# Second block's mixer: two gate products of the convolution ahead of the projections, and an accumulator of its own

## The chip, the cores and the metric

One core of a Trainium2 chip runs the whole program. The metric is device time in microseconds (us) of one execution. TensorE (PE) multiplies matrices and writes to PSUM, VectorE (DVE) and ScalarE (ACT) work on elements, SyncE (SP) issues the transfers. Each engine runs its own queue of instructions in a fixed order and waits on semaphores for the others.

## The reference, cut to what matters

A sequence of 512 frames by 1024 channels goes through three blocks. The second block is a feed-forward layer, a mixer, and another feed-forward layer. Its mixer has two arms that share one projection `p = h @ w_in`:

```python
r, k, v, xw, xa, xg = split(shifted(p[..., :1792]))     # recurrence arm
y = rwkv7_recurrence(rh, wh, kh, vh, -kk, kk * ah)      # 8 heads, state 64 x 64
out_a = (group_norm(y) + bonus) * g
glu = pc[..., :512] * sigmoid(pc[..., 512:])            # convolution arm
c = causal_depthwise_conv(glu, width=31) + conv_b
out_b = silu(layernorm(c))
return concat([out_a, out_b]) @ w_out
```

## The kernel before, in words

**Halves.** The 512 frames are cut into two halves of 256 (`hf` 0 and 1, TH = 256). Every phase is written for the first half and then for the second; the second half uses the same weight tiles. Activations are channel-major tiles of 128 channels by 256 frames. Matrix products use fp16 pairs (high and low part), three matmuls per 128x128 weight tile (`three` and `gemm`, lines 382 to 394; every matmul is issued at line 314), so one output tile of 128 channels costs 24 matmuls of 128x256.

**Weights.** A slot of eight 128x128 tiles (512 KB) is loaded by SP into one of 3 staging tiles, scaled and split by ACT (line 362) and DVE (line 363) into one of 12 ring slots. `m2_s` (14 slots) holds the recurrence's projections, `m2_c` (8 slots) the gate products, `m2_o` (8 slots) the output product.

**Order of work.** The program text is written half by half, but the order on each engine is set when the program is built: a list scheduler takes, among the instructions that are ready in its own model of time, the one with the earliest due time, and the chip then runs each queue in that fixed order. `adv(hf, us)` sets the due time of what follows to the half's clock and moves that clock on; `now` sets it without moving it; the second half's clock lags the first by 22 us in this phase (`LAGS["m2"]`); `boost(us)` makes instructions due earlier, `later(us)` later.

**Buffers.** Tiles come from pools by tag, and tiles of one tag share a fixed number of slots. `m2k` takes from `mid`, 11 slots of 2 KB per partition for each half; `t1k` from `tmp`, 7 slots per half; `b8k` from `big`, one slot per half, which holds the normalised input `hh` (read by all projections and gate products) and afterwards `mix`, the input of the output product. `pmm` and `psmall` are PSUM tiles, two of each per half. A slot is free again when all instructions that name the tile are done.

**The mixer, `mixer2(hf)` (from line 858).** After the norm come 14 projections (loop over `order`, lines 895 to 914): `low` (two tiles of 128 channels, in one slot), then `rkv`, twelve tiles in six slots: two for r, two for k, two for v. Each is copied out by ACT (lines 901, 910) and mixed with the frame before by DVE (lines 911, 912). Then the step list `SEQ[hf]` is played: G0 to G3 are the gate products (`gate_units`: 48 matmuls into `pgl`, a tanh on ACT into `gth` (tag of `t1k`, line 926), the product on DVE into `glu`, line 929), K0 to K3 the convolution of the four channel groups (`convolve`: one DVE instruction at line 939 and 30 at line 941, each reading and rewriting the accumulator). `U`, `P`, `C`, `R`, `B` are the recurrence: `P` (`prep`) makes decay and rate tiles on ACT (`dec`, line 978, tag of `t1k`) and reads k for the last time at line 1002; `C` (`correction`) is a chain of small products `pT` for two chunks of 64 frames; `R` (`chunk`) advances the state, and copies its result to `yt` (`ytok`, a tile of `m2k` for two chunks; ACT, line 1139) from PSUM tile `pxy`; the next chunk's product `pu` needs a PSUM slot of the same tag. K instructions are due 5 us (first half) or 10 us (second) after the half's clock (`CONVL`) and so fill DVE where nothing else is ready.

Before the change the accumulator `cc(j)` is a view of `mix`:

```python
glu, mixed = {}, []
cc = lambda j: mixed[0][:, 4 + j].bitcast(F32).rearrange("p a b -> p (a b)")
```

After the recurrence (lines 1163 on) come the gate `gg` (line 1172), the group norm of `yt` (lines 1177 to 1186, its square `gsq` at line 1181; both `gg` and `gsq` are tiles of `m2k`, `gg` written first in the program), the layer norm of the four `cc` (lines 1200 to 1216) and the output product `po`, which needs all eight 128-channel groups of `mix`: the first four from the recurrence, the last four from the convolution.

Of the kernel before, what the change touches and what calls it, by code (L numbers as in the profile page):

```python
# [10 lines left out]
F32 = mybir.dt.float32  # L11
F16 = mybir.dt.float16
BF = mybir.dt.bfloat16
I32 = mybir.dt.int32
AF = mybir.ActivationFunctionType
OP = mybir.AluOpType
# [3 lines left out]
TH = 256  # L20
D = 1024
KD = 8
FF = 2816
NF = 22
WS = 64.0
# [7 lines left out]
WB = 0  # L33
CB = 80
PB = 10
SEQ = ("G0 G1 G2 G3 K0 K1 K2 K3 U0 P0 U1 P1 C0 R0 R1 C1 R2 R3 B",
       "G0 G1 G2 G3 K0 K1 K2 K3 U0 P0 C0 U1 P1 R0 R1 C1 R2 R3 B")
GB = 20
CONVL = (5, 10)
BOOST = {"norm": 80, "m1f": 80, "m1a": 80, "mix": 80, "m2r": 20, "m2k": 20,  # L40
# [203 lines left out]
def tile_three_blocks(ctx: ExitStack, tc: tile.TileContext, d, col_at, con_at, out, phases=None):  # L244
    nc = tc.nc
    V, S, G, PE = nc.vector, nc.scalar, nc.gpsimd, nc.tensor
# [20 lines left out]
    def adv(hf, us):  # L267
        tc.cur_priority = BASE + int((vt[hf] + lag[hf]) * PER_US)
        vt[hf] += us

    def now(hf):
        tc.cur_priority = BASE + int((vt[hf] + lag[hf]) * PER_US)

    def boost(us=None):
        us = CB if us is None else us
        return tc.high_priority(int(us * PER_US))

    @contextmanager
    def later(us):
        tc.cur_priority += int(us * PER_US)  # L280
        yield
        tc.cur_priority -= int(us * PER_US)
# [6 lines left out]
    def m2k(hf, shape=(128, 512), dt=F32, name="m"):  # L289
        return mid.tile(list(shape), dt, name=name, tag=f"m{hf}")  # L290

    def t1k(hf, shape=(128, TH), dt=F32, name="t"):
        return tmp.tile(list(shape), dt, name=name, tag=f"t{hf}")

    def b8k(hf, shape, dt, name):
        return big.tile(list(shape), dt, name=name, tag=f"b{hf}")

    def kv2k(w, shape=(128, 512), dt=F32, name="kv"):
        return kvp.tile(list(shape), dt, name=name, tag=f"kv{w}")
# [4 lines left out]
    def tiny(hf, n, name="n", dt=F32, p=128):  # L304
        return tin.tile([p, n], dt, name=name, tag=f"{name}{hf}")

    def pmm(hf, shape=(128, 512), dt=F32, name="pm"):
        return psm.tile(list(shape), dt, name=name, tag=f"mm{hf}")

    def psmall(hf, shape=(128, 512), dt=F32, name="pq"):  # L310
        return pss.tile(list(shape), dt, name=name, tag=f"sm{hf}")

    def mm(out_, l, r, start=True, stop=True):
        return PE.matmul(out_, lhsT=l, rhs=r, start=start, stop=stop, skip_group_check=True)  # L314
# [26 lines left out]
    def col(name, i=0, n=1):  # L341
        a, _ = col_at[name]
        return cols[:, a + i:a + i + n]
# [33 lines left out]
    def W(name):  # L377
        if name not in weights:
            weights[name] = Weights(name)
        return weights[name]  # L380

    def three(out_, a, b, first, last, guard):
        (ah, al), (bh, bl) = a, b
        if guard:
            mm(out_, ah, bh, start=first, stop=False)
        with atomic():
            if not guard:
                mm(out_, ah, bh, start=first, stop=False)
            mm(out_, ah, bl, start=False, stop=False)
            mm(out_, al, bh, start=False, stop=last)  # L390

    def gemm(out_, w, i0, nk, x, bank=True):
        for k in range(nk):
            three(out_, w.tile(i0 + k), x(k), bank and k == 0, k == nk - 1, bank and k == 0)
# [3 lines left out]
    def rsqrt(hf, m, y, p=128):  # L398
        shape = list(m.shape)
        n = int(np.prod(shape[1:]))  # L400
        a = t1k(hf, name="rsa") if n > 8 else tin.tile([128, 8], F32, name="rsa", tag=f"rsa{hf}")
        a = a[:shape[0], :n]
        mi, yi = m.bitcast(I32), y.bitcast(I32)
        V.tensor_scalar(yi, mi, 1, None, op0=OP.logical_shift_right)
        V.tensor_scalar(yi, yi, -1.0, float(0x5f3759df), op0=OP.mult, op1=OP.add)
        for _ in range(3):
            V.scalar_tensor_tensor(a, y, -0.5, m, op0=OP.mult, op1=OP.mult)
            V.tensor_tensor(a, a, y, op=OP.mult)
            V.scalar_tensor_tensor(y, a, 1.5, y, op0=OP.add, op1=OP.mult)
# [55 lines left out]
    def pair(hh):  # L465
        return lambda k: (hh[:, 0, k], hh[:, 1, k])
# [389 lines left out]
    m2 = {}  # L856

    def mixer2(hf):
        hh = prenorm(hf, lambda k: col("mpre2", k), None, "m2")
        px = pair(hh)  # L860
        if hf == 0:
# [21 lines left out]
            dw = col("conv_dw", 0, 124)  # L883
# [5 lines left out]
        hv = m2["hv"]  # L889
        prev = m2["prev"]  # L890

        ps = []
        order = [12, 13] + list(range(12))
        sm = {}
        for j in order:
            adv(hf, 2.6)
            p = pmm(hf, [128, TH], name="pp")
            gemm(p, W("m2_s"), j * KD, KD, px)
            with boost(BOOST["m2r"]):
# [12 lines left out]
                V.scalar_tensor_tensor(dst[:, 0:1], prev[:, j:j + 1], col("shift_mu", j), dst[:, 0:1], op0=OP.mult, op1=OP.add)  # L912
                if hf == 0:
                    V.tensor_copy(prev[:, j:j + 1], raw[:, TH - 1:TH])

        glu, mixed = {}, []
        cc = lambda j: mixed[0][:, 4 + j].bitcast(F32).rearrange("p a b -> p (a b)")

        def gate_units(j):
            adv(hf, 5.2)  # L920
            p = pmm(hf, [128, 2, TH], name="pgl")
            gemm(p[:, 0], W("m2_c"), 16 * j, KD, px)
            gemm(p[:, 1], W("m2_c"), 16 * j + 8, KD, px, bank=False)
            with boost(GB):
                t = t1k(hf, name="gth")
                S.activation(t, p[:, 1], AF.Tanh, scale=0.5 / WS)
                glu[j] = gl = m2k(hf, [128, TH + 30], F32, "glu")
                V.tensor_copy(gl[:, 0:30], m2["hist"][:, j, 0:30])
                V.scalar_tensor_tensor(gl[:, 30:], t, 1.0, p[:, 0], op0=OP.add, op1=OP.mult)
                if hf == 0:  # L930
                    V.tensor_copy(m2["hist"][:, j, 0:30], gl[:, TH:TH + 30])

        def convolve(j):
            if not mixed:
                mixed.append(b8k(hf, [128, KD, 2, TH], F16, "mix"))
            gl, dw = glu[j], m2["dw"]
            now(hf)
            with later(CONVL[hf]):
                V.tensor_scalar(cc(j), gl[:, 0:TH], dw[:, j * 31:j * 31 + 1], col("conv_b", j), op0=OP.mult, op1=OP.add)
                for i in range(1, 31):  # L940
                    V.scalar_tensor_tensor(cc(j), gl[:, i:i + TH], dw[:, j * 31 + i:j * 31 + i + 1], cc(j),  # L941
                                           op0=OP.mult, op1=OP.add)

        xwa, xg = sm[12], sm[13]
        rr = lambda p_: ps[p_ // 2][:, p_ % 2]
        kk_ = lambda p_: ps[2 + p_ // 2][:, p_ % 2]
# [1 line left out]
        with boost(BOOST["m2k"]):  # L948
# [7 lines left out]
            for q in range(4):  # L956
                t = t1k(hf, name="ksq")
# [184 lines left out]
        with boost(BOOST["m2k"]):  # L1142
            for step in SEQ[hf].split():
                n = int(step[1:] or 0)
# [16 lines left out]
        now(hf)  # L1161
        vt[hf] += HOLD["m2"]
        with boost(BOOST["m2c"]):
            mix = mixed[0]

            gup = kv2k(0, name="gup")
            nc.sync.dma_start(out=gup, in_=d["m2_gup"])
            gg = [m2k(hf, [128, 2, TH], F32, "gg") for _ in range(2)]
            for q in range(4):
                p = pmm(hf, [128, TH], name="pw")  # L1170
                mm(p, gup[:, q * 128:(q + 1) * 128], xg)
                S.activation(gg[q // 2][:, q % 2], p, AF.Copy)

            for tt in range(2):
                y = ytok[tt]
                mu = tiny(hf, 8, "gmu")
                V.tensor_reduce(mu, y, axis=AX.X, op=OP.add)
                V.tensor_scalar(mu, mu, 1.0 / 64, None, op0=OP.mult)
                V.tensor_tensor(y, y, mu[:, :, None].to_broadcast([128, 8, 64]), op=OP.subtract)
                sq = m2k(hf, [128, 8, 64], F32, "gsq")  # L1180
                S.activation(sq, y, AF.Square)
                vr, rs_ = tiny(hf, 8, "gvr"), tiny(hf, 8, "grs")
                V.tensor_reduce(vr, sq, axis=AX.X, op=OP.add)
                V.tensor_scalar(vr, vr, 1.0 / 64, 64e-5, op0=OP.mult, op1=OP.add)
                rsqrt(hf, vr, rs_)
                V.tensor_tensor(y, y, rs_[:, :, None].to_broadcast([128, 8, 64]), op=OP.mult)
                p = psmall(hf, [128, 4, 128], name="pch")
                y2 = y.rearrange("p h c -> p (h c)")
                c_ = slice(tt * 128, (tt + 1) * 128)
                for q in range(4):  # L1190
                    PE.transpose(p[:, q], y2[:, q * 128:(q + 1) * 128], ident)
                for q in range(4):
                    t = t1k(hf, [128, 128], name="oa")
                    S.activation(t, p[:, q], AF.Identity, scale=col("gn_w", q), bias=col("gn_b", q))
                    V.tensor_tensor(t, t, vv(q)[:, c_], op=OP.add)
                    V.tensor_tensor(t, t, gg[q // 2][:, q % 2, c_], op=OP.mult)
                    split(hf, mix[:, q, 0, c_], mix[:, q, 1, c_], t)
        with boost(BOOST["m2n"]):
# [11 lines left out]
            for j in range(4):  # L1210
                t = t1k(hf, name="cn")
# [289 lines left out]
```

## Time and profile before

| what | value |
|---|---|
| median of 3 runs | 3496.53 us (3487.12 to 3506.42) |
| the profiled execution | 3507.87 us |
| its span, first to last instruction | 3506.0 us |
| mean granted TensorE clock | 0.980 of 2.4 GHz |
| weight transfers in the mixer | `m2_s` x14, `m2_c` x8, `m2_o` x8, 512.0 KB each, 3.5 to 3.6 us from issue to landing |

The rows below come from the profiled execution, whose time is 11.3 us over the median. Busy times are unions over a stretch: an instruction's own duration overlaps the next one's on the same engine, so a run of instructions is shorter than the sum of its durations. Times in rows are us from the start of the span. An engine's idle time is followed in brackets by what ended it.

### The profile page before, as it was taken

What the parts mean: (1) busy time and instruction counts of PE and PEld (TensorE: products, weight loads), DVE (VectorE), ACT (ScalarE), POOL (GpSimd) and SP (SyncE); (2) the same over time, 40 slices, a digit from 0 to 9 for tenths busy, and PEclk for the clock granted to TensorE, in tenths of its full rate; (3) what the DMA queues carried; (4) which work ended last, traced back from release to release, by engine and by line L of the source; (5) the groups of instructions that cost most, each with busy time, mean ns of one, the idle gap of its engine ahead of it and who ended that gap; (6) DMA issues with size and microseconds to landing.
All of it is one profiled execution on the core that took longest, in us unless ns stands there. A gap on an engine that the chain in (4) does not pass through costs nothing. (4 is left out here: it accounts for less than half of the span.)

```text
span 3506.0 us, 71986 instructions
## 1 busy us (share of the span) xinstructions
PE 3309.1 (94%) x30164; PEld 2815.7 (80%) x30164; DVE 2171.3 (62%) x5240; ACT 1545.5 (44%) x3335; POOL 19.1 (1%) x24
## 2 busy tenths in 40 slices
PE   5999999999999999997789999889999998999998
PEld 5888867788888888886678887667888876688887
DVE  8953768844374437688884438887544488855433
ACT  3332466433343324424243326886433278853331
POOL 0000000000000000000000000000000000000000
PEclk9999999999999999987889999999999999999999
DMA  8932313232323332201023323112233321123331
GB/s 276 326 110 91 118 55 130 67 103 97 99 96 102 104 97 91 70 5 34 4 89 104 102 97 99 55 43 67 85 104 102 105 85 51 41 80 109 103 99 47
DMA packets 105591, 327.89 MB, mean 94 GB/s; under 512 B 12584, under 2 KB 18088, under 8 KB 105008
## 3 DMA queue, kind: packets, MB, share of 16 engines
q1 hardware_dynamic: 105264, 323.28, 28.1%
q8 instruction: 236, 3.87, 0.5%
q14 instruction: 91, 0.75, 0.1%
HBM read 321.14 MB, written 2.10 MB: 92 GB/s over the span
## 5 line engine op out<-in xcount | busy, mean ns | idle before, releaser
L314 PEld LDWEIGHTS <-wr 128*128 128x128 f16 x24000 | 2351.0, 99 | 327.8 <-issue 25.5
L314 PE MATMUL pgu<-hh,wr 128*128 128x256 f16 x12672 | 1402.6, 273 | 7.9 <-ACT wr L362 2.3
L363 DVE SCALAR_TENSOR_TENSOR wr<-st,wr 128x1024 f16<-128x1024 f32 x524 | 640.3, 1223 | 353.3 <-ACT wr L362 344.0
L314 PE MATMUL po<-act,wr 128*128 128x256 f16 x6336 | 702.0, 273 | 0.1
L362 ACT ACTIVATE wr<-st 128x1024 f16<-128x1024 f32 x524 | 552.2, 1055 | 323.2 <-PE pgu L314 128.3
L314 PE MATMUL pp<-hh,wr 128*128 128x256 f16 x3072 | 384.1, 274 | 4.8 <-DVE rot L1261 2.2
L523 ACT ACTIVATE fth<-pgu 128x256 f32<-128x256 f32 x264 | 101.3, 384 | 590.4 <-PE pgu L314 590.2
L524 DVE SCALAR_TENSOR_TENSOR fth<-fth,pgu 128x256 f32<-128x256 f32 x264 | 111.0, 420 | 355.9 <-ACT fth L523 355.8
L314 PE MATMUL po<-mix,wr 128*128 128x256 f16 x1536 | 198.0, 282 | 15.9 <-ACT mix L444 9.0
L444 ACT ACTIVATE act<-fac 128x256 f16<-128x256 f32 x264 | 110.2, 417 | 174.1 <-DVE fac L526 173.8
L314 PE MATMUL pt<-wr,hh 128*128 128x512 f16 x576 | 145.4, 383 | 1.6 <-DVE wr L363 1.6
L445 DVE TENSOR_TENSOR act<-fac,act 128x256 f16<-128x256 f32 x264 | 111.3, 422 | 50.5 <-ACT act L444 50.0
L492 DVE TENSOR_TENSOR acc<-acc,sq 128x256 f32<-128x256 f32 x84 | 35.4, 421 | 149.5 <-ACT sq L491 149.5
L1260 ACT ACTIVATE rsw<-pp 32x256 f32<-32x256 f32 x304 | 114.3, 376 | 19.6 <-PE pp L314 15.3
L432 ACT ACTIVATE sq<-x 128x256 f32<-128x256 f32 x154 | 56.5, 411 | 134.0 <-DVE x L501 129.6
L526 DVE SCALAR_TENSOR_TENSOR fac<-fth,pgu 128x256 f32<-128x256 f32 x264 | 110.8, 420 | 7.7
L485 ACT ACTIVATE y<-po 128x256 f32<-128x256 f32 x64 | 24.5, 383 | 204.8 <-PE po L314 204.7
L941 DVE SCALAR_TENSOR_TENSOR mix<-glu,cols,mix 128x256 f32<-128x256 f32 x240 | 102.2, 477 | 0.1
L314 PEld LDWEIGHTS <-hh 128*128 128x128 f16 x768 | 62.2, 100 | 48.3 <-issue 3.2
L619 DVE TENSOR_REDUCE amx<-ps 128x1 f32<-128x128 f32 (+3 forms) x160 | 77.3, 487 | 34.4 <-PE ps L314 32.6
L565 DVE SCALAR_TENSOR_TENSOR ada<-adw,csil,ada 128x512 f32<-128x512 f32 x126 | 91.0, 747 | 5.8 <-DMA adw<-in_w_ada_dram 5.6
L501 DVE SCALAR_TENSOR_TENSOR x<-po,x 128x256 f32<-128x256 f32 x64 | 26.9, 422 | 108.1 <-PE po L314 108.0
(356 smaller groups left out, 2935.6 us busy)
## 6 DMA issues: line engine op xcount, KB each, us to landing
st<-in_gu_dram SPq DMA_DIRECT2D x264, 512.0 KB, 3.5
st<-in_dn_dram SPq DMA_DIRECT2D x132, 512.0 KB, 3.5
adw<-in_w_ada_dram SPq DMA_DIRECT2D x144, 256.0 KB, 5.2
st<-in_m_o_dram SPq DMA_DIRECT2D x32, 512.0 KB, 3.6
st<-in_m_b_dram SPq DMA_DIRECT2D x16, 512.0 KB, 3.6
st<-in_m_a_dram SPq DMA_DIRECT2D x16, 512.0 KB, 3.8
st<-in_m_s_dram SPq DMA_DIRECT2D x14, 512.0 KB, 3.6
st<-in_m_qk_dram SPq DMA_DIRECT2D x8, 512.0 KB, 4.0
```

Of the source, the lines that this page charges most:

```text
L314: return PE.matmul(out_, lhsT=l, rhs=r, start=start, stop=stop, skip_group_check=True)
L362: S.activation(r[:, 0], st, AF.Copy, scale=WS)
L363: V.scalar_tensor_tensor(r[:, 1], st, WS, r[:, 0], op0=OP.mult, op1=OP.subtract)
L444: S.activation(hi, src, AF.Copy)
L445: V.tensor_tensor(lo, src, hi, op=OP.subtract)
L523: S.activation(t, p[:, 0], AF.Tanh, scale=0.5 / WS)
L524: V.scalar_tensor_tensor(t, t, 1.0, p[:, 0], op0=OP.add, op1=OP.mult)
L526: V.scalar_tensor_tensor(a, t, 0.5 / WS / WS / AS, p[:, 1], op0=OP.mult, op1=OP.mult)
L565: V.scalar_tensor_tensor(ada_acc[g, h], src, csil[:, k:k + 1], ada_acc[g, h], op0=OP.mult, op1=OP.add)
L619: V.tensor_reduce(nm, s[:, :nk], axis=AX.X, op=OP.max, negate=True)
L941: V.scalar_tensor_tensor(cc(j), gl[:, i:i + TH], dw[:, j * 31 + i:j * 31 + i + 1], cc(j), op0=OP.mult, op1=OP.add)
L1260: S.activation(sw[a:a + 32], p[c:c + 32], AF.Copy, scale=scale)
```

## The change: what it does

G0 and G1 leave the step list and are made by a plain loop before the 14 projections. `gate_units` and `convolve` move up in the text with them, unchanged but for the accumulator. `cc(j)` is now half of a tile of `m2k` (tag of `mid`), one tile for K0 and K1 and one for K2 and K3, asked for when the first of the two is written down. `mix` is asked for after the recurrence instead of at the first convolution. The pools keep their sizes.

```diff
-SEQ = ("G0 G1 G2 G3 K0 K1 K2 K3 U0 P0 U1 P1 C0 R0 R1 C1 R2 R3 B",
-       "G0 G1 G2 G3 K0 K1 K2 K3 U0 P0 C0 U1 P1 R0 R1 C1 R2 R3 B")
+SEQ = ("G2 G3 K0 K1 K2 K3 U0 P0 U1 P1 C0 R0 R1 C1 R2 R3 B",
+       "G2 G3 K0 K1 K2 K3 U0 P0 C0 U1 P1 R0 R1 C1 R2 R3 B")
...
+        glu, ccs = {}, {}
+
+        def cc(j):
+            if j // 2 not in ccs:
+                ccs[j // 2] = m2k(hf, [128, 2, TH], F32, "cc")
+            return ccs[j // 2][:, j % 2]
+
+        def gate_units(j):
+            adv(hf, 5.2)
...
+        def convolve(j):
+            gl, dw = glu[j], m2["dw"]
...
+        for j in range(2):
+            gate_units(j)
+
         ps = []
         order = [12, 13] + list(range(12))
...
-        glu, mixed = {}, []
-        cc = lambda j: mixed[0][:, 4 + j].bitcast(F32).rearrange("p a b -> p (a b)")
-
-        def gate_units(j):
...
-        def convolve(j):
-            if not mixed:
-                mixed.append(b8k(hf, [128, KD, 2, TH], F16, "mix"))
...
         with boost(BOOST["m2c"]):
-            mix = mixed[0]
+            mix = b8k(hf, [128, KD, 2, TH], F16, "mix")
```

## Rows read from the trace of the kernel before

**Rows 1.** The page's first part: busy us, share, instructions by engine.

```profile
PE 3309.1 (94%) x30164; PEld 2815.7 (80%) x30164; DVE 2171.3 (62%) x5240; ACT 1545.5 (44%) x3335; POOL 19.1 (1%) x24
```

**Rows 2.** Stretches: length, busy us of PE, PEld, DVE, ACT, POOL; clock, DMA, GB/s.

```profile
1390.00:1462.00 72.00, 72.00 (x644) 62.52 (x643) 36.62 (x92) 32.76 (x65) 0.00 (x0) 1.00 0.26 87
1484.00:1555.00 71.00, 70.54 (x1358) 60.18 (x1358) 65.46 (x169) 17.76 (x37) 0.00 (x0) 1.00 0.04 10
1591.00:1655.00 64.00, 46.12 (x627) 35.94 (x626) 55.44 (x200) 31.48 (x78) 0.00 (x0) 0.76 0.13 42
1655.00:1722.00 67.00, 66.73 (x997) 55.98 (x997) 56.04 (x140) 17.32 (x40) 0.00 (x0) 1.00 0.02 6
1722.00:1774.00 52.00, 23.37 (x102) 16.14 (x101) 47.60 (x162) 17.54 (x44) 0.00 (x0) 0.62 0.17 51
```

**Rows 3.** Timeline of VectorE: the last run of convolution instructions, second half.

```profile
1742.09 7.61 DVE L941 SCALAR_TENSOR_TENSOR mix<-glu,cols,mix 128x256 f32<-128x256 f32 x19
```

**Rows 4.** Timeline of TensorE: the second half's output product starts, then goes on.

```profile
1739.44 5.19 PE L314 MATMUL po<-mix,wr 128*128 128x256 f16 x24 [2.19 <-ACT mix L444]
...
1769.65 5.43 PE L314 MATMUL po<-mix,wr 128*128 128x256 f16 x24 [2.90 <-ACT mix L444]
```

**Rows 5.** Groups by line, 1300 to 1850 us: busy us, mean ns of one, idle before.

```profile
L941 DVE SCALAR_TENSOR_TENSOR mix<-glu,cols,mix 128x256 f32<-128x256 f32 x240 | 102.2, 477 | 0.1
L314 PE MATMUL pp<-hh,wr 128*128 128x256 f16 x672 | 76.6, 273 | 0.0
L314 PE MATMUL pgl<-hh,wr 128*128 128x256 f16 x384 | 48.2, 273 | 0.0
...
L911 DVE SCALAR_TENSOR_TENSOR rkv<-raw,cols,rkv 128x255 f32<-128x255 f32 x24 | 11.5, 479 | 2.4 <-ACT rkv L910 2.1
```

**Rows 6.** Timeline of TensorE: a product of `prep`, first half, into PSUM.

```profile
1430.05 0.48 PE L314 MATMUL pw<-low,wau 64*128 64x128 f32 x2
```

**Rows 7.** Timeline of ScalarE: last gate tanh and first decay, first half.

```profile
1462.12 0.38 ACT L926 ACTIVATE gth<-pgl 128x256 f32<-128x256 f32 x1 [3.51 <-PE pgl L314]
1462.40 0.36 ACT L978 ACTIVATE dec<-pw,halved 128x128 f32<-128x128 f32 x1
```

**Rows 8.** Timeline of VectorE: the group norm's subtraction, chunks 0 and 1, second half.

```profile
1679.92 0.69 DVE L1179 TENSOR_TENSOR yt<-yt,gmu 128x512 f32<-128x512 f32 x1
```

**Rows 9.** Timeline of ScalarE, second half: gate copies and the square after them.

```profile
1723.30 0.82 ACT L1172 ACTIVATE gg<-pw 128x256 f32<-128x256 f32 x2 [0.79 <-PE pw L314]
...
1725.19 0.62 ACT L1181 ACTIVATE gsq<-yt 128x512 f32<-128x512 f32 x1
```

**Rows 10.** Timeline of VectorE: `prep`'s last reads of k's first slot; first convolution run.

```profile
1480.67 0.29 DVE L1002 TENSOR_TENSOR rate<-rate,rkv 128x128 f32<-128x128 f32 x1
...
1494.99 0.47 DVE L941 SCALAR_TENSOR_TENSOR mix<-glu,cols,mix 128x256 f32<-128x256 f32 x1
...
1652.80 0.29 DVE L1002 TENSOR_TENSOR rate<-rate,rkv 128x128 f32<-128x128 f32 x1
```

**Rows 11.** Stretches of the instructions on `glu` alone: VectorE busy (count), clock, DMA.

```profile
1627.00:1653.00 26.00, 6.73 (x15) 0.67 0.20 66
1653.00:1669.00 16.00, 2.29 (x5) 1.00 0.08 19
1669.00:1700.00 31.00, 18.52 (x45) 1.00 0.01 2
1700.00:1714.00 14.00, 6.69 (x16) 1.00 0.01 2
```

**Rows 12.** Timeline of ScalarE: copies to `yt` of chunks 0, 1 and 2, second half.

```profile
1668.58 0.59 ACT L1139 ACTIVATE yt<-pxy 64x512 f32<-64x512 f32 x1 [0.29 <-PE pxy L314]
...
1677.04 0.59 ACT L1139 ACTIVATE yt<-pxy 64x512 f32<-64x512 f32 x1 [2.20 <-PE pxy L314]
...
1713.06 0.60 ACT L1139 ACTIVATE yt<-pxy 64x512 f32<-64x512 f32 x1 [1.19 <-PE pxy L314]
```

**Rows 13.** Timeline of TensorE: chunk 2 starts, second half, after its correction.

```profile
1700.69 1.99 PE L314 MATMUL pA<-zb 64*128 64x128 f32 x16
```

More of the change, by code (lines that the diff above doesn't have):

```diff
@@ L890, in mixer2 @@
         prev = m2["prev"]
+        glu, ccs = {}, {}
[5 more added lines that the diff above has]
+            adv(hf, 5.2)
+            p = pmm(hf, [128, 2, TH], name="pgl")
+            gemm(p[:, 0], W("m2_c"), 16 * j, KD, px)
+            gemm(p[:, 1], W("m2_c"), 16 * j + 8, KD, px, bank=False)
+            with boost(GB):
+                t = t1k(hf, name="gth")
+                S.activation(t, p[:, 1], AF.Tanh, scale=0.5 / WS)
+                glu[j] = gl = m2k(hf, [128, TH + 30], F32, "glu")
+                V.tensor_copy(gl[:, 0:30], m2["hist"][:, j, 0:30])
+                V.scalar_tensor_tensor(gl[:, 30:], t, 1.0, p[:, 0], op0=OP.add, op1=OP.mult)
+                if hf == 0:
+                    V.tensor_copy(m2["hist"][:, j, 0:30], gl[:, TH:TH + 30])
+        def convolve(j):
+            gl, dw = glu[j], m2["dw"]
+            now(hf)
+            with later(CONVL[hf]):
+                V.tensor_scalar(cc(j), gl[:, 0:TH], dw[:, j * 31:j * 31 + 1], col("conv_b", j), op0=OP.mult, op1=OP.add)
+                for i in range(1, 31):
+                    V.scalar_tensor_tensor(cc(j), gl[:, i:i + TH], dw[:, j * 31 + i:j * 31 + i + 1], cc(j),
+                                           op0=OP.mult, op1=OP.add)
+        for j in range(2):
+            gate_units(j)
         ps = []
@@ L914, in mixer2 @@
                     V.tensor_copy(prev[:, j:j + 1], raw[:, TH - 1:TH])
-        glu, mixed = {}, []
-        cc = lambda j: mixed[0][:, 4 + j].bitcast(F32).rearrange("p a b -> p (a b)")
-        def gate_units(j):
[L920 to L931, printed above, removed]
-        def convolve(j):
-            if not mixed:
-                mixed.append(b8k(hf, [128, KD, 2, TH], F16, "mix"))
[L936 to L942, printed above, removed]
         xwa, xg = sm[12], sm[13]
```

## The prediction

> **What bounds the kernel now.** First the page: TensorE is busy 94% of the span [rows 1], so a gain must come out of a stretch where it waits. Then the stretches of the second block's mixer [rows 2]. In 1390 to 1462 us TensorE is full (72.00 of 72.00) with projections and gate products, and VectorE is idle for 72.00 - 36.62 = 35.4 us. In 1591 to 1655 TensorE is idle for 64 - 46.12 = 17.9 us. In 1722 to 1774 it is busy only 23.37 of 52 at clock 0.62, while VectorE has 47.60 of 52: here VectorE holds the kernel up. Then what ends that last wait: the convolution of the second half runs as 19 instructions without a gap until 1742.09 + 7.61 = 1749.70 [rows 3], that is 0.40 us each. The second half's output product starts on the recurrence's channels at 1739.44, must then wait for the convolution's, and goes on at 1769.65 [rows 4]. So the stage ends 20.0 us (the layer norm) after the last convolution instruction. The question is where the change puts those instructions.
>
> **A rule that the trace shows.** Slots of one tag are given out in the order of the program, even when later requests are ready. A product of `prep` was in PSUM by 1430.5 [rows 6], yet `dec`, which reads such a product, ran only at 1462.40, right behind the tanh of the fourth gate product at 1462.12 [rows 7]; `gth` stands ahead of `dec` in the program and takes the same tag. Again: the group norm's subtraction was done at 1679.92 + 0.69 = 1680.6 [rows 8], but its square `gsq` ran at 1725.19, behind `gg` at 1723.30 [rows 9], which asks for the same tag earlier in the program. I take this as the rule.
>
> **The change part by part.**
>
> *Work.* Nothing goes and nothing comes: eight gate products and 4 x 31 convolution instructions per half remain. The accumulator is another tile of the same shape and type (0.48 us each before [rows 5]): 0.
>
> *Two products moved ahead.* One takes 48.2 / 8 = 6.0 us, a projection 76.6 / 28 = 2.7 us [rows 5]. Two products, 12.0 us, pass 14 projections on a full TensorE [rows 2]: same work in another order, 0. On SP's queue four `m2_c` slots pass fourteen `m2_s` slots of the same 512 KB, one slot used in each 2.7 to 3.0 us either way: 0. POOL's queue has none of this. The recurrence does not start later, as `dec` waits for the fourth product in both orders [rows 7]. In the second half 12.0 / 2.7 = 4.4 projections slide behind the first half's last product into 1484 to 1555, where they fill TensorE instead of gate products. Their evacuation costs VectorE 4.4 x 0.48 = 2.1 us of the 71 - 65.46 = 5.5 us idle there [rows 2, 5], and ACT has 17.76 of 71. I take 0, bound +2.1: what they push back is the first half's convolution, which ends in a stretch with idle on every engine.
>
> *Its own accumulator.* This is meant to free the convolution from `mix`, which could only be had when the last product had read `hh`. But the tag has 11 slots, and ahead of the first `cc` the program asks for `glu` 0 and 1, `low`, six `rkv`, `glu` 2 and 3: 11. By the rule `cc` is the twelfth and needs a release. `glu` 0 cannot be released first (the convolution reads it); `low`, r and v live to the end of the recurrence; only k goes earlier, when `prep` has read it. First half: k's first slot is free at 1480.67, and before the change the convolution's run began at 1494.99 anyway, VectorE being taken by `prep` [rows 10]: 0. Second half: `P1` stands behind `C0`, k's slot is free at 1652.80 [rows 10], and by then the kernel before had done 15 convolution instructions (1627 to 1653 [rows 11]). These move behind: 15 x 0.40 = 6.0 us. Lower end 0, if they fit in the 67 - 56.04 = 11 us of idle VectorE in 1655 to 1722 [rows 2]; below that -6.0, if `C0` and `P1`, which they no longer delay in 1627 to 1653, gain their whole length. I take +6.0: in 1655 to 1722 convolution work was already waiting beside that idle time and did not fill it, and the tail is gapless [rows 3].
>
> *The new wait.* `cc` takes both slots of k, so `yt` must wait for `glu` 0 and 1, that is for the end of K0 and K1 (31 instructions each). The copy to `yt` of chunk 0 stood at 1668.58 [rows 12]. At the pace before, K0 has 5 instructions by 1669 and 26 of the next 45 [rows 11]: done at 1669 + 31 x 26 / 45 = 1687. Behind that copy wait ACT's queue and chunk 1's `pu`, which needs the PSUM slot. Chunk 1 takes 8.5 us from copy to copy (to 1677.04 [rows 12]), so it ends near 1695.5; chunk 2 cannot start before its correction is done, 1700.69 [rows 13]. The correction covers the wait with 5 us to spare: 0. K1 ends at 1700 + 14 x (62 - 50) / 16 = 1710.5, before the copy of chunk 2 at 1713.06: 0. If either cover is gone, each us late is 1 us of the recurrence, of which the convolution's tail hides the first ones; bound +4.
>
> **Sum.** 0 + 0 + 6.0 + 0 = +6.0 us. On the profiled execution 3507.87 + 6.0 = 3513.9; that one lies 11.3 over the median of 3496.5, so the forecast for a median is 3502.5. The unknowns make it -6.0 to 6.0 + 2.1 + 4 = +12.1, and runs before spread by 10 us to each side: 3480 to 3519 as its own range. About 0.5% (17.5 us) is what a measurement can tell from no change, so this counts as no change.
>
> **Rivals.**
>
> *Faster: `cc` gets a slot at once.* If slots went to whoever is ready, K0 and K1 of both halves would run in the 35.4 us of idle VectorE (88 instructions at 0.40 [rows 2, 3]), the tail of rows 3 would be gone, and the output product would go on at 1739.44 + 5.19 = 1744.6 instead of 1769.65 [rows 4]: -25.0. With the first half's convolution early too, its output product could fill up to 17.9 us of 1591 to 1655 [rows 2]: -43. So 3453 to 3472, middle 3462. For it: the idle time is real. Against it: both cases of the rule, and the count of 11. The Trainium skill (Perfetto Trace Analysis, Optimization Strategy) says that where the most-contended engine changes over time, interleaving the regimes may help; by that advice this rival is what a TensorE stretch beside a VectorE stretch calls for. The trace has the two regimes [rows 2], but no run here shows them interleaved. Chance 0.15.
>
> *Slower: K0 and K1 gate the recurrence.* If the second half's K instructions, due late, are placed behind the correction instead of between its steps, or the waiting `yt` copy blocks the correction's own copies on ACT, chunk 1 and chunk 3 wait for them in series: the 26 remaining of K0 and 31 of K1 cost 57 x 0.40 = 22.8 us (the 6.0 are among them): 3519.3. It decides from the point where K0 ends after 1700.69 - 8.5 = 1692 us. For it: only 5 us of cover. Against it: before, 45 such instructions did run between the correction's steps [rows 11]. Chance 0.18.
>
> *The new tile does nothing at all:* the 15 instructions fit in idle time, 3496.5. That lies in the forecast's own range and is counted with it: 0.64 for both. 0.03 is left for the unforeseen.
>
> **How the numbers follow.** Faster by over 0.5%: the first rival, 0.15, and 0.02 of the rest. Slower: the second, 0.18, and 0.04 from the forecast's upper end and the rest. Same: 0.61. The range takes in the forecast's own and the slower rival (3519.3 and a few us), and reaches down to the smallest gain of the faster one, 3471: to 3522.
>
> **What would show it.** Right: the first convolution instruction of each half stands behind `prep`'s read of k's first slot (line 1002), VectorE stays about half idle while TensorE is full with projections, the copies to `yt` of chunks 0 and 2 in the second half follow K0's and K1's last instruction, and the second half's output product goes on some 20 us after the last convolution instruction, about 6 us later than before. Wrong: convolution instructions of the first half among the projections (the first rival), or TensorE idle between chunk 0 and chunk 1 of the second half with the correction done (the second). If the projections that slide back slow the first half's recurrence by more than 2 us, the price of the moved products is wrong.

## The result: slower by 0.7%

| kernel | median, us | runs | ratio to the kernel before, 95% interval |
|---|---|---|---|
| before | 3499.24 (3487.12 to 3517.75) | 11 | |
| after | 3527.11 (3521.90 to 3534.12) | 11 | 1.007 (1.005 to 1.009) |

The forecast was 3502.5 us, range 3471 to 3522, no change likeliest. The profiled execution of after has a span of 3523.5 us against 3506.0. The mean granted clock of TensorE does not account for it by itself: at the same 0.980, the six runs of after on record took 3521.90 to 3527.54 us, the seven of before 3507.87 to 3514.89.

**The profile after.** The page's first part has the same work as [rows 1], so the loss is waiting:

```profile
PE 3302.9 (94%) x30157; PEld 2812.3 (80%) x30164; DVE 2175.9 (62%) x5240; ACT 1544.8 (44%) x3335; POOL 19.1 (1%) x24
```

The stretches of after, columns as in [rows 2]:

```profile
1390.00:1462.00 72.00, 72.00 (x644) 62.52 (x643) 35.93 (x91) 32.89 (x64) 0.00 (x0) 1.00 0.27 84
1655.00:1704.00 49.00, 48.67 (x782) 41.10 (x781) 43.18 (x115) 13.73 (x32) 0.00 (x0) 1.00 0.03 8
1704.00:1728.00 24.00, 2.42 (x23) 1.97 (x22) 24.00 (x62) 0.88 (x4) 0.00 (x0) 0.59 0.00 0
1728.00:1761.00 33.00, 27.32 (x222) 22.68 (x222) 24.06 (x82) 7.68 (x19) 0.00 (x0) 0.68 0.00 1
1820.00:1860.00 40.00, 31.20 (x253) 26.38 (x251) 29.20 (x85) 15.01 (x33) 0.00 (x0) 0.87 0.13 42
```

Two of the same stretches before:

```profile
1704.00:1728.00 24.00, 20.47 (x195) 16.17 (x192) 17.95 (x45) 6.65 (x15) 0.00 (x0) 0.99 0.00 1
1820.00:1860.00 40.00, 40.00 (x369) 35.85 (x367) 22.27 (x45) 15.81 (x30) 0.00 (x0) 1.00 0.24 80
```

Beside the projections (first line of after) VectorE is as idle as before: no convolution moved there. The third line is new: for 24 us TensorE does 2.42 us of work while VectorE is full. The last line is a second new hole, far behind the mixer. ScalarE's timeline names the first wait, the copies to `yt` of the second half:

```profile
1727.89 0.59 ACT L1143 ACTIVATE yt<-pxy 64x512 f32<-64x512 f32 x1 [20.78 <-DVE cc L919]
1734.76 0.59 ACT L1143 ACTIVATE yt<-pxy 64x512 f32<-64x512 f32 x1 [2.90 <-PE pxy L314]
1752.29 0.59 ACT L1143 ACTIVATE yt<-pxy 64x512 f32<-64x512 f32 x1 [3.18 <-PE pxy L314]
1760.90 0.59 ACT L1143 ACTIVATE yt<-pxy 64x512 f32<-64x512 f32 x1 [0.64 <-PE pxy L314]
```

The first stood at 1668.58 before [rows 12], the last at 1721.92. The first now waits for a convolution instruction, of which VectorE's timeline has one gapless run at that time:

```profile
1703.63 25.41 DVE L919 SCALAR_TENSOR_TENSOR cc<-glu,cols,cc 128x256 f32<-128x256 f32 x64
```

That run ends at 1729.04, 1.2 us behind the copy: `yt` waits not for 31 instructions of K0 but for nearly all 124 of the half. The copy is released three instructions (0.40 us each) ahead of the run's end. I read from it that the four convolutions take turns on VectorE's queue, one instruction each, so that the first ends almost with the last. The view of the tile `cc` gives the sum, both halves:

```profile
who waited for it (us, times):
  ACT yt L1143: 28.1, 2
```

TensorE's timeline of after shows what stands behind the copy, and where its queue goes on:

```profile
1705.59 0.83 PE L314 MATMUL po<-mix,wr 128*128 128x256 f16 x6
1728.53 1.11 PE L314 MATMUL pu<-xx,tt 64*64 64x64 f32 x14 [22.12 <-ACT yt L1143]
...
1760.80 0.39 PE L314 MATMUL pgu<-hh,wr 128*128 128x256 f16 x2
...
1793.79 4.29 PE L314 MATMUL po<-mix,wr 128*128 128x256 f16 x24 [2.96 <-ACT mix L444]
1798.51 5.40 PE L314 MATMUL po<-mix,wr 128*128 128x256 f16 x48 [0.42 <-ACT acc L488]
1803.74 5.40 PE L314 MATMUL pgu<-hh,wr 128*128 128x256 f16 x48
1808.98 5.40 PE L314 MATMUL po<-mix,wr 128*128 128x256 f16 x48
1814.22 5.40 PE L314 MATMUL pgu<-hh,wr 128*128 128x256 f16 x48
1819.46 5.40 PE L314 MATMUL po<-mix,wr 128*128 128x256 f16 x48
```

The second half's output product goes on at 1793.79 instead of 1769.65 [rows 4], 24.1 us late. And there is a change that the prediction has no word on: `pgu`, the next layer's products of the first half, now stand between and ahead of the second half's output tiles; before, all eight output tiles came first:

```profile
1775.40 7.36 PE L314 MATMUL po<-mix,wr 128*128 128x256 f16 x66 [0.32 <-ACT acc L488]
...
1791.51 2.46 PE L314 MATMUL po<-mix,wr 128*128 128x256 f16 x21
1793.80 4.34 PE L314 MATMUL pgu<-hh,wr 128*128 128x256 f16 x34
```

With those products used up, TensorE has nothing ahead of it when it must wait for the second half's norm: the hole at 1820 to 1860 (31.20 busy of 40; before, 40.00).

Both kernels run TensorE full from 1860 on for 140 us, so the loss can be read where the third block starts, at the first projection behind 2100 us, before and then after:

```profile
2149.27 1.47 PE L314 MATMUL pp<-hh,wr 128*128 128x256 f16 x12
```

```profile
2169.13 1.47 PE L314 MATMUL pp<-hh,wr 128*128 128x256 f16 x12
```

That is 19.9 us, all of the loss of the span (17.5). The experiments below are read at this mark too.

### The profile page after: what moved, and what is told of

It is laid out like the page before. It is cut to its first block, busy times and chain, and to the rows that moved or that the text cites. A ratio compares the mean times of both kernels' runs of the same rounds, so it can differ in the third digit from the quotient of the medians.

```text
span 3523.5 us, 72005 instructions
## 1 busy us (share of the span) xinstructions
PE 3302.9 (94%) x30157; PEld 2812.3 (80%) x30164; DVE 2175.9 (62%) x5240; ACT 1544.8 (44%) x3335; POOL 19.1 (1%) x24
## 5 line engine op out<-in xcount | busy, mean ns | idle before, releaser
L492 DVE TENSOR_TENSOR acc<-acc,sq 128x256 f32<-128x256 f32 x84 | 35.4, 421 | 156.8 <-ACT sq L491 156.8
L919 DVE SCALAR_TENSOR_TENSOR cc<-glu,cols,cc 128x256 f32<-128x256 f32 x240 | 99.0, 476 | 0.1
```

## The experiments

Each run was timed in five rounds beside the kernel before. "Mark" is the start of that projection in the one profiled execution, less 2149.27.

| run | what it has of the change | mark, us | ratio, 95% interval |
|---|---|---|---|
| only_products | products early, `cc` in `mix` | -0.2 | 0.9996 (0.9978 to 1.0014) |
| only_tile | `cc` tiles, products in place | +20.6 | 1.0075 (1.0047 to 1.0104) |
| yt_mix | all, but `yt` has no wait | +19.0 | 1.0068 (1.0045 to 1.0091) |
| k_order | all, convolutions one after another | +25.2 | 1.0067 (1.0041 to 1.0092) |
| yt_mix_po | as yt_mix, old TensorE order | +8.9 | 1.0054 (1.0031 to 1.0076) |
| after_po | all, output products together | +12.0 | 1.0043 (1.0024 to 1.0061) |
| before_late10 | none; a TensorE order like after's | +16.6 | 1.0076 (1.0047 to 1.0105) |
| early_po | first `cc` early, `yt` in `mix` | -18.5 | 0.9949 (0.9929 to 0.9969) |
| gate | products early, late start alone | -0.3 | 1.0006 (0.9984 to 1.0028) |
| early | as early_po, old due times | -16.8 | 0.9966 (0.9946 to 0.9986) |
| early_po_l20 | as early_po, K0 and K1 due later | -22.7 | 0.9932 (0.9910 to 0.9955) |
| early_wb | as early_po, weights due earlier | -28.8 | 0.9930 (0.9908 to 0.9952) |
| hold | slots claimed, `cc` in `mix` | +19.7 | 1.0075 (1.0056 to 1.0095) |
| hold_po | as hold, output products together | +7.8 | 1.0073 (1.0046 to 1.0099) |
| before_wb | none; weights and output products due earlier | +6.9 | 1.0006 (0.9985 to 1.0028) |
| early_wb_l20 | early_wb and early_po_l20 | -31.6 | 0.9938 (0.9917 to 0.9958) |

One execution is not a median: before_wb's mark is 6.9 us late in an execution of 3513.12 us, while its runs reach from 3490.73 to 3518.02, and hold_po's was taken in the fastest of its six runs (3513.02 us; median 3524.80). The executions also differ ahead of what was changed: before_late10 differs from before only behind the recurrence, yet its last copy to `yt` stands 6.7 us earlier (1715.26 for 1721.92). So a few us of a mark by itself say nothing.

**Which half of the change?** only_products puts the accumulator back into `mix`; only_tile leaves the products in the step list.

```diff
 # only_products
-                ccs[j // 2] = m2k(hf, [128, 2, TH], F32, "cc")
+        cc = lambda j: mixed[0][:, 4 + j].bitcast(F32).rearrange("p a b -> p (a b)")
 # only_tile
-        for j in range(2):
-            gate_units(j)
```

> The two gate products still go ahead of the projections, but the accumulator is a view of mix again, as in the kernel before. Theory A (the loss is the copy to yt, which waits for glu's slots until the convolution is nearly done; the moved products are free): within 6 us of the kernel before, 3493 to 3505, and the second half's copies to yt stand within 4 us of 1668.6 and 1713.1. Rival B (the moved products themselves cost the 28 us, by pushing the projections of the second half back): about 3527. Rival C (the loss is the convolution's late start, 15 instructions behind prep): as A here, since the accumulator has its old place.

> The accumulator takes tiles of the mid pool as in the changed kernel, but all four gate products stay in the step list, behind the projections. Theory A: the requests ahead of cc are still 11, cc takes k's slots, yt waits for glu's; so nearly the whole loss stays: 3518 to 3532, and the first copy to yt of the second half waits for an instruction on cc for 15 us or more. Rival B (moved products): about 3499, as the kernel before. Rival C (late start): as A in time, but with no wait of yt on cc.

The products cost nothing and gain nothing; the tile carries the whole loss.

**Is it `yt`'s wait?** yt_mix gives `yt` the place in `mix`; k_order makes the four convolutions due one after another.

```diff
 # yt_mix
-                ytok.append(m2k(hf, [128, 8, 64], F32, "yt"))
+                ytok.append(mixed[0][:, 4 + c:6 + c].bitcast(F32)...)
 # k_order
-            with later(CONVL[hf]):
+            with later(CONVL[hf] + 6 * j):
```

> The changed kernel, but yt is a view of the place in mix that the accumulator held before (its last four channel groups), so that it asks for no slot of mid; cc still takes k's slots, and the moved products stay moved. Theory A: the wait of yt is gone and what is left is the 15 displaced convolution instructions of the prediction: 3497 to 3508, TensorE's idle time of 22 us ahead of pu gone. Rival B (moved products): still about 3527. Rival C (late start of the convolution costs the 28 us): still about 3520 to 3527, with the last convolution instruction of the second half 15 us or more behind 1749.7.

> The changed kernel, but the four convolutions of a half are due one after the other, 6 us apart, and not all at one time. Theory A with its round robin (in the changed kernel the four run in turn, so the first ends nearly as late as the last): now the first ends after about its own 31 instructions, near 1690 in the second half as the prediction took it, its slot is free, and most of the stall goes: 3500 to 3513, the copy to yt of chunk 0 in the second half before 1700. Rival D (the order of the four is of no matter; what holds yt is that VectorE has no time for 31 more instructions until the recurrence stalls): still 3520 to 3530, with that copy behind 1715.

Theory A falls as the whole account. In yt_mix the second half's copies to `yt` stand at 1670.02 to 1723.32, as before the change, and the loss is the same. In k_order ScalarE idles only 1.7 us for `cc` in all, but the first copy to `yt` now stands behind the correction's copies on ScalarE's queue, at 1704.19, between what theory A (before 1700) and rival D (behind 1715) expected; the convolution ends only at 1784.8 and the output product goes on at 1797.81. TensorE's timeline of yt_mix shows where its time went:

```profile
1774.34 5.34 PE L314 MATMUL po<-mix,wr 128*128 128x256 f16 x24 [2.90 <-ACT mix L444]
...
1795.71 21.41 PE L314 MATMUL pgu<-hh,wr 128*128 128x256 f16 x192
1816.95 5.40 PE L314 MATMUL po<-mix,wr 128*128 128x256 f16 x48
...
1844.95 25.29 PE L314 MATMUL pgu<-hh,wr 128*128 128x256 f16 x216 [1.02 <-ACT hh L444]
```

So taking the wait away did bring the output product forward, from 1793.79 to 1774.34, only 4.7 us later than before. But its last two tiles stand behind four units (192 matmuls) of the next layer and end at 1822, for 1825 in after and 1794 before: what was won at the copy is lost again in TensorE's order. That order was fixed when the program was built. I read it as the scheduler's model seeing the convolution some us late too, so that the next layer's first-half products, due earlier, were ready ahead of the last output tiles; no run shows the model's own times.

**Is it TensorE's order?** The output products of the second half are made due 40 us earlier (yt_mix_po, after_po), or 10 us later in the kernel before (before_late10). Their copies out and sums of squares move with them; the norm that follows keeps its due time.

```diff
+        vt[1] -= 40 * hf
         acc = out_tiles(hf, W("m2_o"), KD, ...)
+        vt[1] += 40 * hf
```

> As the run with yt in mix, and the second half's output products are due 40 us earlier, which puts all eight on TensorE's queue ahead of the next layer's first products, as in the kernel before; nothing else moves. Theory E (two causes, either of which is enough for the loss: yt's wait, and the queue order, in which the last output products of the second half stand behind products of the next layer, so that TensorE later stands before the second half's norm with the first half's products behind it): with both gone 3498 to 3509, and TensorE full in 1820 to 1860. Rival F (neither; something else of the new tile costs it, the late convolution above all): still 3518 to 3527.

> The changed kernel with the second half's output products due 40 us earlier; yt still waits for glu's slots. Theory E: the 24 us by which the second half's output product goes on late stay, but the next layer's first-half products now cover the norm behind it: 3508 to 3519, between the two kernels. If the queue order is the whole loss, 3498 to 3507; if yt's wait is, 3520 to 3530.

> The kernel before with the second half's output products due 10 us later, so that on TensorE's queue the last of them stand behind the next layer's first products; the convolution, its tiles and yt are untouched. Theory E: the queue order alone costs 12 to 26 us, 3511 to 3526, with TensorE idle about 8 us in 1820 to 1860. Rival F: within 6 us of the kernel before, 3493 to 3506.

before_late10 settles one thing: with convolution, `yt` and slots as before, the order alone costs as much as the whole change. Two lines of its order on TensorE, then its stretch behind the mixer (before, 40.00 of TensorE's 40):

```profile
1796.31 13.26 PE L314 MATMUL pgu<-hh,wr 128*128 128x256 f16 x120
...
1817.02 3.44 PE L314 MATMUL po<-mix,wr 128*128 128x256 f16 x30
```

```profile
1820.00:1860.00 40.00, 25.87 (x195) 21.08 (x193) 29.61 (x85) 14.10 (x29) 0.00 (x0) 0.79 0.19 56
```

The other two divide the theories: after_po's median, 3517.64 us, lies in the 3508 to 3519 of theory E, but yt_mix_po's, 3518.43, at the lower end of rival F's 3518 to 3527 and not in E's 3498 to 3509. At the mark the old order gives back 10.1 us (yt_mix to yt_mix_po) and 7.9 us (after to after_po, where two units of the next layer still stand ahead of the tiles), but not all, and the intervals of the ratios overlap. In times it shows between after and after_po: ten of after_po's eleven runs are faster than the fastest of after's.

**Is it the late start, or the slots?** gate makes the convolution's first instructions read a small tile that is asked for in `cc`'s place and released at once; hold keeps two such tiles until the layer norm, as long as `cc` lives. In both the accumulator stays in `mix`.

```diff
 # gate
+                gate.append(m2k(hf, [128, 4], F32, "gate"))
-                V.tensor_scalar(cc(j), ..., col("conv_b", j), ...)
+                V.tensor_scalar(cc(j), ..., gate[0][:, j:j + 1], ...)
 # hold (its tile holds conv_ln_w too, read where cn is made)
+                hold.append(m2k(hf, [128, 2, TH], F32, "hold"))
```

> The two products go ahead, the accumulator stays a view of mix, and the output products stay ahead of the next layer's; but the convolution's first instructions read their bias from a small tile of the mid pool that is asked for where the changed kernel asks for cc, so that the convolution cannot start before k's slot is free. This is the displaced start alone (+6.0 in the prediction). Theory G (the late start costs 6 to 9 us on TensorE's way to the third block): the third block's first projection 6 to 9 us later than in the kernel before, 3505 to 3512. Rival H (what is left in the runs with the order put back is not the late start but another trait of the new tile): within 3 us of the kernel before, there and in time (3496 to 3506).

> The accumulator stays a view of mix; but two small tiles of the mid pool are asked for exactly where the changed kernel asks for cc, are read by the convolution's first instructions and by the layer norm's last ones, and so hold k's slots as long as cc does. This is the slot claim alone. Theory J (the slot claim is the whole loss; where the accumulator lies is of no matter): as the changed kernel, third block's first projection within 3 us of 2169.1, 3518 to 3530. Rival K (the new place itself costs part): 8 us or more less than the changed kernel, third block's first projection before 2161.

> The slot claim alone, with the second half's output products due 40 us earlier so that all eight stand ahead of all but two of the next layer's products. Theory J: as after_po, third block's first projection within 3 us of 2161.2, 3508 to 3520. Rival K: within 5 us of the kernel before.

hold is the changed kernel over again, in time, at the mark, in the first copy to `yt` (1727.83) and in TensorE's order of output tiles and next layer's products: where the accumulator lies is of no matter, the claim on two slots is the whole loss. hold_po was expected at 3508 to 3520 us; its median is 3524.80, with three runs at 3513 to 3517 and three at 3532 to 3534, so that it does not repeat after_po's gain in time. gate behaves as the kernel before, which is what its rival H expected. ScalarE's and TensorE's timelines of hold:

```profile
1727.83 0.59 ACT L1148 ACTIVATE yt<-pxy 64x512 f32<-64x512 f32 x1 [21.07 <-DVE mix L924]
```

```profile
1803.64 5.40 PE L314 MATMUL pgu<-hh,wr 128*128 128x256 f16 x48
1808.88 5.40 PE L314 MATMUL po<-mix,wr 128*128 128x256 f16 x48
```

VectorE's and then TensorE's timeline of gate:

```profile
1741.56 12.35 DVE L922 SCALAR_TENSOR_TENSOR mix<-glu,cols,mix 128x256 f32<-128x256 f32 x31
...
1754.17 0.47 DVE L922 SCALAR_TENSOR_TENSOR mix<-glu,cols,mix 128x256 f32<-128x256 f32 x1
```

```profile
1770.33 5.34 PE L314 MATMUL po<-mix,wr 128*128 128x256 f16 x24 [2.90 <-ACT mix L444]
```

The convolution ends at 1754.64, 4.9 us later than in [rows 3], as the prediction's +6.0 has it; yet the output product goes on 0.7 us later than in [rows 4]. The gap between the two was 20.0 us and is now 15.7: before the change VectorE scaled four weight slots (1.22 us each) between the last convolution instruction and the layer norm's subtraction, here one.

**A version that gives the convolution its slot at once.** The first `cc` is asked for and K0 and K1 are written right behind the first two products; the fourth product moves behind `prep`, so that its `glu` and the second `cc` take k's slots; `yt` lies in `mix`. All but early have the output products due 40 us earlier too, and so has before_wb, which its expectation leaves out.

```diff
-SEQ = ("G2 G3 K0 K1 K2 K3 U0 P0 U1 P1 C0 R0 R1 C1 R2 R3 B",
-       "G2 G3 K0 K1 K2 K3 U0 P0 C0 U1 P1 R0 R1 C1 R2 R3 B")
+SEQ = ("G2 U0 P0 U1 P1 G3 C0 K2 K3 R0 R1 C1 R2 R3 B",
+       "G2 U0 P0 C0 U1 P1 G3 K2 K3 R0 R1 C1 R2 R3 B")
...
         for j in range(2):
             gate_units(j)
+        for j in range(2):
+            convolve(j)
 # early_wb, early_wb_l20 and before_wb
-WBS = {"m2_o": 0, "gu22": 0}
+WBS = {"m2_o": 0, "gu22": 0, "m2_s": 20, "m2_c": 20}
 # early_po_l20 and early_wb_l20
+            with later(CONVL[hf] + 20 * (j < 2)):
```

> The version that gives the convolution a slot at once: the first cc tile is asked for right behind the first two gate products and K0 and K1 are written there; the fourth gate product is made behind prep, so that its glu and the second cc take k's slots; yt lies in mix; the second half's output products are due 40 us earlier. Theory E: K0 and K1 run in VectorE's idle time beside the projections, the convolution of the second half ends by 1725 and the output product goes on by 1750: 3475 to 3495. Rival (the fourth product's late place or the recurrence's own chain takes over as the bound): 3496 to 3515.

> The version with the early slot, but with the output products' due times as in the kernel before. By the queue order theory: some 8 to 17 us of the gain are lost again, 3487 to 3500. If the order matters only where the convolution is late: as with the due times moved, 3475 to 3488.

> The version with the early slot and the output products due earlier, where K0 and K1 are due 20 us later than there, behind the scaling of the weights on VectorE. If the 7 us in which TensorE waited for scaled weights in 1410 to 1460 came from the convolution's place on VectorE's queue, they go: 3470 to 3481. If the convolution only moves into the recurrence's time and delays that, 3482 to 3492.

> The version with the early slot and the output products due earlier, where the mixer's projection and gate weights are loaded and scaled 20 us earlier in due time instead. If VectorE's queue order is what made TensorE wait for weights, 3470 to 3481; if the staging tiles or the ring have no room for an earlier load, no change, 3478 to 3488.

> The kernel before with the mixer's projection and gate weights due 20 us earlier and nothing else. If the early version's gain is the earlier convolution, this gains little: 3493 to 3504. If the weights were the gain, 3475 to 3488.

> The early version with the weights due 20 us earlier and K0 and K1 due 20 us later. If what is left of TensorE's waits beside the projections comes from the convolution on VectorE's queue, a further gain, 3465 to 3476; if the convolution then runs into the recurrence, no gain or a loss, 3476 to 3486.

All five early versions beat both kernels; early_wb is 0.7% faster than the kernel before (0.9908 to 0.9952). before_wb says that the earlier weights and output products gain nothing without the early convolution; TensorE's order of output tiles is there that of before. early, with the old due times, is at 3490.44 us against early_po's 3481.83, as the order theory has it, but their intervals overlap. early_po, early_po_l20, early_wb and early_wb_l20 cannot be told apart. Two stretches of before and of early_wb:

```profile
1390.00:1480.00 90.00, 89.87 (x753) 73.84 (x751) 52.00 (x168) 46.24 (x103) 0.00 (x0) 1.00 0.22 71
1655.00:1780.00 125.00, 95.77 (x1144) 76.83 (x1145) 108.85 (x313) 40.17 (x99) 0.00 (x0) 0.84 0.08 25
```

```profile
1390.00:1480.00 90.00, 86.86 (x751) 70.42 (x750) 87.37 (x280) 42.57 (x98) 0.00 (x0) 0.98 0.20 63
1655.00:1780.00 125.00, 104.21 (x1213) 86.10 (x1212) 90.82 (x266) 47.64 (x110) 0.00 (x0) 0.86 0.10 34
```

Beside the projections VectorE has 35.4 us more to do; in the recurrence's stretch 18.0 us less, and TensorE 8.4 us more. In the changed kernel that stretch holds 108.36 us of VectorE work, as many as before it: the change took nothing out. I read from this that the early versions gain by work taken out of the stretch; in early_wb the output product goes on at 1753.57 and its last tile ends at 1774.12, for 1769.65 and 1793.97 before. The sum does not explain the loss, though: gate has 108.48 us there and loses nothing.

## Why the prediction was wrong, by its own steps

- **What bounds before the change, and the rule of the slots: right.** `cc` was the twelfth request and got k's slots, the first convolution instructions of the second half standing behind `prep`; nothing moved into the projections.
- **Two products moved ahead, 0 (bound +2.1): right.** only_products is at 0.9996. The fourth product's tanh came at 1462.58 and 1550.62 (before, 1462.12 [rows 7] and 1554.33), so `dec` was not held up.
- **Its own accumulator, +6.0: right as a delay, wrong as a price.** gate shows 4.9 us at the last convolution instruction and nothing at the third block. The sum took it that the stage ends 20.0 us after that instruction. In after this instruction ends at 1729.04, 20.7 us earlier than before, and the output product goes on 64.8 us behind it: the recurrence, held by the new wait, came last there, not the convolution.
- **The new wait, 0 (bound +4): this step failed.** "K0 has 5 instructions by 1669 and 26 of the next 45 [rows 11]: done at 1669 + 31 x 26 / 45 = 1687" gives K0 more than half of the convolution's instructions. Four convolutions with one due time share VectorE in turn; by that pace K0 is done with the whole lot. The copy came at 1727.89, and the recurrence's last copy 39.0 us late (1760.90 for 1721.92). The correction's cover, done at 1700.8 as foretold, was never what decided.
- **What is missing altogether: the scheduler's answer on another engine.** The prediction let TensorE's queue order stand. The claim on two slots turned it (hold has after's order, gate that of before), and before_late10 shows that such an order alone can cost 0.76%.
- **The slower rival (3519.3, chance 0.18): right in place and in sign.** K0 and K1 gate the recurrence, TensorE is idle ahead of chunk 1's `pu` with the correction done. Its +22.8 us is close to the 19.9 at the mark and inside the ratio's 17.5 to 31.5 us, but for a reason it did not have: its sum was 57 instructions in series, while yt_mix has the same loss with no such wait. That the sizes agree is luck.
- **The faster rival (3462, 0.15) was the right picture of another change.** Where `cc` does get its slot at once, early_wb stands at 3477.92 us. The advice of the Trainium skill (Perfetto Trace Analysis, Optimization Strategy) to interleave regimes whose contended engine differs holds in these runs, by 0.7%; the change did not reach it, for want of a free slot.

Not settled: how the loss divides in the changed kernel. The slot claim makes `yt` wait and turns TensorE's order. Three pairs differ only in the due times of the output products. Read from the recurrence's last copy to the mark, which leaves out what differs ahead of it, the old order gives back 8.6 us (after to after_po), 11.2 (yt_mix to yt_mix_po) and 8.9 (hold to hold_po); in before_late10 the turned order costs 23.2. That is one execution of each, and in the ratios after_po and hold_po do not differ from after and hold by more than their intervals. Without either of the two, yt_mix_po still has +8.9 us at the mark (1.0054). There the recurrence's last copy is 2.5 us late, the last convolution instruction 7.2, the output product 5.8 where it goes on and 8.2 at its last tile's end; that the late convolution is the whole of the 8.9 is argued, not shown.

## What to carry to other kernels

Before a tile is moved into a pool, list the requests of its tag in program order and ask of each later one whose last reader it now waits for; when that reader is one of several equal chains with one due time, count the end of all of them. A wait that fills the timeline with idle time is not yet the bound: put it out of the way, and if the time stays, follow what it released to the place where that waits again. Where a scheduler fixes the queues, compare their order behind the change on every engine: 10 us on one due time turned an order here, which cost 0.76%.

## What had not been expected of the hardware

A chain of dependent VectorE instructions is slower than chains in turn. In early_po's second half the last two convolutions run one behind the other, and VectorE's timeline has gapless runs in which every instruction needs the one ahead of it:

```profile
1680.54 3.60 DVE L919 SCALAR_TENSOR_TENSOR cc<-glu,cols,cc 128x256 f32<-128x256 f32 x7
...
1686.68 4.12 DVE L919 SCALAR_TENSOR_TENSOR cc<-glu,cols,cc 128x256 f32<-128x256 f32 x8
```

With 0.48 us for the last, that is (4.12 - 0.48) / 7 = 0.52 us from one to the next; in after's run of 64, where four chains take turns, it is (25.41 - 0.48) / 63 = 0.40 us. So the turns that made K0 late also make the whole convolution shorter.
